# A hybrid decoder layer: condition rows ahead of the second broadcast, inputs written rounded, weights cast by GpSimd, four idle products

## The chip, the cores and the metric

The kernel runs on one core of one Trainium2 chip. The metric is the device time of one execution in microseconds, lower is better. The engines are PE (matrix products, with PEld for its weight loads), DVE (vector), ACT (scalar), POOL (GpSimd) and SP, whose queue issues the transfers.

## The reference

One layer of a hybrid decoder is applied to a prompt of 1024 tokens and to 32 sample tokens (8 sequences of 4). What the change touches is the beginning: the normalised input, scaled and shifted by rows that come from a condition vector, and its product with the input weights.

```python
def adaln_in(x, c, w_ada, b_ada, g_norm):
    mod = jax.nn.silu(c) @ w_ada + b_ada
    shift, scale, gate = jnp.split(mod, 3, axis=-1)
    h = rmsnorm(x, g_norm) * (1 + scale[:, None, :]) + shift[:, None, :]
    return h, gate[:, None, :]

def layer(x, c, ...):
    h, gate = adaln_in(x, c, w_ada, b_ada, g_norm)
    (mq, mk, mv, mi, mf, mo, mz, aq, ak, av, az, gm, ga) = split_in(h @ w_in)
    y_m, C, n, m = mlstm_branch(mq, mk, mv, mi, mf, mo, mz, ...)
    ...   # sliding-window attention of aq, ak, av gives y_a
    u = jax.nn.sigmoid(gm) * (y_m @ w_mo) + jax.nn.sigmoid(ga) * (y_a @ w_ao)
    return x + gate * (u @ w_o), ...
```

## The kernel before

The input is kept transposed: eight tiles of 128 rows of the model dimension (index k), in three parts by token: part 0 and part 1 of 512 prompt tokens each (`xT[0]`, `xT[1]`) and part 2, the 32 sample tokens (`xS`). The products run over three pieces of columns of the same tokens: 384, 384 and 288, so that piece 1 needs parts 0 and 1, and piece 2 needs part 1 and the samples.

The beginning goes as follows. `x_sq` squares the tiles (ACT or DVE) and adds the squares with products against ones (`xs`); `x_cols` brings the sums into columns (`xc`); `x_rs` forms the reciprocal root on DVE with a chain of small instructions (`xr`); `x_dg` makes diagonal tiles of it (`xdg`); `x_rows` broadcasts them over all rows by a product with ones (`xb`); `x_mul` multiplies the input by that. Beside this, the condition is multiplied by four chunks of `w_ada`, each of which serves two values of k. `ada_chunk` is a generator in steps: eight products (`ada_q`), an ACT copy of the result (`adas_q`), four small products that transpose it (`adat_q`), and `tokens_done`, which writes the scale A and the shift B on DVE.

`h_part(k, p)` then writes x*A+B on ACT, a rounded copy of it (the high half `h_h`), and on DVE the difference (the low half `h_l`). `h_samples` does the same for the samples. `split4` splits a weight tile into halves `wh` and `wl` alike. `pair(ks, p, accs)` runs the products of the first two jobs, `ak` and `av`, for piece p: for each k and job three products, high with high, high weight with low input, low weight with high input. The loop over `two` takes k in four groups of two; in each group it forms the inputs, runs the pieces 0, 1 and 2, and steps the next condition chunk in between. After it come the gate products (`gg`) and the rest of the layer.

The order on PE, DVE and ACT is the order in which the program is written: each instruction is tied to the one before it on its engine. POOL and SP are in program order as well, except that a planner moves an instruction to where its tile is free. The raw weights of the two jobs have nine tiles, and the transfers share eight semaphores, so an issue on SP waits until the one eight places ahead has landed.

Of the kernel before, what the change touches and what calls it, by code (L numbers as in the profile page):

```python
# [10 lines left out]
F32 = mybir.dt.float32  # L11
# [4 lines left out]
ALU = mybir.AluOpType  # L16
# [156 lines left out]
def body(tc, a):  # L173
    nc = tc.nc
    with ExitStack() as ctx:
# [14 lines left out]
        def po(shape, name):  # L190
            return ps.tile(shape, F32, tag="o", bufs=2, name=name)
# [61 lines left out]
        def mm(out, lhsT, rhs, start, stop, share=1, more=False):  # L253
            n = int(np.prod(rhs.shape[1:]))
            side.now += max(n, 250) / 2400 if rhs.dtype == F32R else max(n * 4 // share, 128) / 2400
            side.products += 1
            in_order(nc.tensor.matmul(out, lhsT, rhs, start=start, stop=stop, skip_group_check=more))  # L257
# [117 lines left out]
        def x_sq(cols, j, p, ks, on_v=(), apart=KT):  # L375
            n = PARTS[p][1]
            if p == 2:
                sqs = ht([128, KT, NS], "xsq2")
                S.activation(sqs, xS, AF.Square)
                for k in ks:  # L380
                    columns(cols, j, n, sqs[:, k], one[:, 0:1], k == 0, k == KT - 1)
                return
            for k in ks:
                if k == 0:
                    sums[p] = po([128, 512], f"xs{p}")
                sq = ht([128, 512], "xsq")
# [57 lines left out]
        def h_part(k, p):  # L444
            x = xT[p][k]
            hi, lo = h_hi(k, *PARTS[p]), h_lo(k, *PARTS[p])
            S.activation(x, x, AF.Identity, bias=B[:, k, 0:1], scale=A[:, k, 0:1])
            if k < 6:
                S.copy(hi, x)
            else:  # L450
                V.tensor_copy(hi, x)
            V.tensor_tensor(lo, x, hi.bitcast(F32), op=ALU.subtract)

        def h_samples(ks):
            ks = slice(ks[0], ks[-1] + 1)
            xv = xS[:, ks].rearrange("p k (b t) -> p k b t", t=NT)
            for i, m in enumerate((A, B)):
                V.tensor_tensor(xv, xv, m[:, ks, 1:9].unsqueeze(3).to_broadcast((128, ks.stop - ks.start, NB, NT)),
                                op=(ALU.mult, ALU.add)[i])
            hi, lo = (f(ks, SEQ, NS) for f in (h_hi, h_lo))  # L460
            V.tensor_copy(hi, xS[:, ks])
            V.tensor_tensor(lo, xS[:, ks], hi.bitcast(F32), op=ALU.subtract)


        def granule(name, tag, bufs, dt=F32):
# [9 lines left out]
                dma(raws[-1], src[:, 4 * i:4 * i + 4], late)  # L475
            return raws, name

        def split4(raw, name, eng=V):
            hi, lo = granule(f"wh_{name}", "wh", 4, F32R), granule(f"wl_{name}", "wl", 4, F32R)
            S.copy(hi, raw)  # L480
            eng.tensor_tensor(lo, raw, hi.bitcast(F32), op=ALU.subtract)
            return hi, lo

# [1076 lines left out]
        def pair(ks, p, accs):  # L1560
            c0, n = PIECES[p]
            for k in ks:
                for job_, acc in zip(order[:2], accs):
                    wh, wl = ready[job_]
                    o = acc[:, :n]
                    mm(o, wh(k), h_hi(k, c0, n), start=(k == 0), stop=False)
                    mm(o, wh(k), h_lo(k, c0, n), start=False, stop=False)
                    mm(o, wl(k), h_hi(k, c0, n), start=False, stop=(k == KT - 1))

        def pair_end(p, accs):  # L1570
            c0, n = PIECES[p]
            ev_ak(p, accs[0], c0, n)
            ev_av(p, accs[1], c0, n)

        two = [range(k, k + 2) for k in range(0, KT, 2)]

# [8 lines left out]
                dma(raws1[n][i], a["w1"][JOBS[n]][:, 4 * i:4 * i + 4])  # L1585

        def first_split(n, i, eng):
            parts1[n].append(split4(raws1[n][i], f"{n[0]}0_{i}", eng))
            ready[n] = tuple((lambda k, j=j: parts1[n][k // 4][j][:, k % 4]) for j in range(2))

        adas = [tokens_ada(0, "h0")]
# [1 line left out]
        adas += [tokens_ada(1, "h1"), tokens_ada(2, "l1")]  # L1593
        first_load(1)
        adas.append(tokens_ada(3))
        xc0, xc1 = po([128, 8], "xc0"), po([128, 8], "xc1")
        xc0, xc1 = pg([128, 8], "xc0"), pg([128, 8], "xc1")
        x_sq(xc0, 4, 2, range(KT))
        x_sq(xc0, 0, 0, range(KT), (1, 3, 5, 7))
        x_sq(xc1, 0, 1, range(4), (1, 3))  # L1600
        conditions()
        x_cols(xc0, 0)
        dgs = x_dg((0, 2), *x_rs((0, 2), xc0))
        x_sq(xc1, 0, 1, range(4, KT))
        x_cols(xc1, 1)
        rows = {p: x_rows(p, dgs[p]) for p in (0, 2)}
        dgs = x_dg((1,), *x_rs((1,), xc1), True)
        x_mul(2, rows[2], None)
        x_mul(0, rows[0], two[0])
        steps(adas[0], 3)  # L1610
        rows[1] = x_rows(1, dgs[1])
        kept = ht([128, 512], "xbs")
        S.copy(kept, rows[1])
        x_mul(0, rows[0], two[1])
        run(adas[0])
        first_split(order[0], 0, V)
        x_mul(1, kept, two[0][:1])
        acc = [(pg([128, 384], "g_ak0"), po([128, 384], "g_av0")),
               (po([128, 384], "g_ak1"), pg([128, 384], "g_av1")),
               (pa([128, 384], "g_ak2"), pa([128, 384], "g_av2"))]  # L1620
        for q, kk in enumerate(two):
            more = q < len(two) - 1
            if q == 2:
                attention_begin()
                wg, gbias = gate_load()
                preload(order[2])
                dma(cst[:, C_TRI:], a["cst"][:, C_TRI:])
            h_part(kk[0], 0)
            if q == 0:
                first_split(order[1], 0, V)  # L1630
            h_part(kk[1], 0)
            if q == 0:
                x_mul(1, kept, kk[1:])
            if q and more:
                steps(adas[q + 1], 2)
            pair(kk, 0, acc[0])
            if q == 0:
                steps(adas[1], 2)
            h_part(kk[0], 1)
            if q and more:  # L1640
                steps(adas[q + 1], 1)
            h_part(kk[1], 1)
            if q == 0:
                steps(adas[1], 1)
                x_mul(0, rows[0], range(4, KT))
            h_samples(kk)
            if not more:
                pair_end(0, acc[0])
                prefetch(order[2])
            pair(kk[:1], 1, acc[1])  # L1650
            if more:
                run(adas[q + 1])
            pair(kk[1:], 1, acc[1])
            if more:
                x_mul(1, kept, two[q + 1])
            else:
                pair_end(1, acc[1])
            pair(kk, 2, acc[2])
            if q == 0:
                for n in order[:2]:  # L1660
                    first_split(n, 1, V)
        pair_end(2, acc[2])
        zg = []
        for p, (c0, n) in enumerate(PARTS):
# [270 lines left out]
```

## Time and profile before

| what | value |
|---|---|
| median of 3 runs | 856.53 us (855.49 to 857.94) |
| the profiled execution, its own time | 854.31 us |
| its span | 852.5 us |
| busy share of PE, DVE, ACT, POOL | 97%, 67%, 45%, 4% |
| share of PE in the chain that ended last | 93% |
| DMA share from 0 to 62 us | 0.96 |
| granted PE clock from 0 to 62 us | 0.97 |

The span is the profiled execution from its first to its last instruction; its own time is longer by what lies around it. In a timeline each row has a start, a duration, the engine, the line of the program, the operation, and in brackets the idle time of the engine before it with what ended it. Since every operation of DVE and ACT is issued by one helper (line 219) and every product by another (line 257), groups are told apart by the names of tiles. A product in f32 has two records, so the eight products of a condition chunk show as x16. The granted clock is the share of the full clock that the throttle let through.

### The profile page before, as it was taken

What the parts mean: (1) busy time and instruction counts of PE and PEld (TensorE: products, weight loads), DVE (VectorE), ACT (ScalarE), POOL (GpSimd) and SP (SyncE); (2) the same over time, 40 slices, a digit from 0 to 9 for tenths busy, and PEclk for the clock granted to TensorE, in tenths of its full rate; (3) what the DMA queues carried; (4) which work ended last, traced back from release to release, by engine and by line L of the source; (5) the groups of instructions that cost most, each with busy time, mean ns of one, the idle gap of its engine ahead of it and who ended that gap; (6) DMA issues with size and microseconds to landing.
All of it is one profiled execution on the core that took longest, in us unless ns stands there. A gap on an engine that the chain in (4) does not pass through costs nothing.

```text
span 852.5 us, 15278 instructions
## 1 busy us (share of the span) xinstructions
PE 829.6 (97%) x5248; PEld 697.5 (82%) x5248; DVE 569.5 (67%) x1619; ACT 386.7 (45%) x987; POOL 30.9 (4%) x63
## 2 busy tenths in 40 slices
PE   6899999999999999999999999999999999999996
PEld 2689989789788988888888777777778999987785
DVE  4877785555675785656655656787877657756586
ACT  4762356546565554555444444444445232223231
POOL 0000000000000000000000000000002112220000
PEclk9999999999999999999999999999999999999998
DMA  9996548348637655273423443554435888353502
GB/s 329 361 318 226 144 141 292 108 114 292 193 92 234 171 186 170 83 226 91 137 99 110 133 131 101 147 173 125 125 112 177 267 288 301 124 160 111 174 25 80
DMA packets 114321, 146.48 MB, mean 172 GB/s; under 512 B 27088, under 2 KB 70992, under 8 KB 114212
## 3 DMA queue, kind: packets, MB, share of 16 engines
q1 hardware_dynamic: 114244, 145.52, 53.5%
q8 instruction: 41, 0.67, 0.3%
q14 instruction: 36, 0.29, 0.1%
HBM read 107.50 MB, written 38.99 MB: 172 GB/s over the span
## 4 chain that ended last, share of the span: by engine, by line
PE 93%; DVE 3%; ACT 2%; DMA 1%; issue 1%; SPq 0%; DVEq 0%
PE fo L257 11%; PE bx L257 11%; PE by L257 10%; PE bw L257 10%; PE g_aq L257 6%; PE g_w_mo L257 5%; PE bz L257 5%; PE g_w_ao L257 5%; PE g_mq L257 4%; PE g_mk L257 3%; PE g_mv L257 3%; PE sc L257 2%; PE smp L257 2%; PE oT L257 2%; PE g_ak L257 2%; PE pt L262 1%
## 5 line engine op out<-in xcount | busy, mean ns | idle before, releaser
L257 PE MATMUL g_w_ao<-ya,wh_w_ao 128*128 128x384 f32 (+1 forms) x192 | 45.6, 322 | 0.1
L257 PE MATMUL g_w_mo<-ym_l,wh_w_mo 128*128 128x384 f32 (+1 forms) x192 | 45.7, 323 | 0.0
L219 ACT ACTIVATE p<-p,nmx 128x256 f32<-128x256 f32 (+1 forms) x64 | 31.1, 488 | 20.6 <-DVE nmx L219 20.6
L219 ACT ACTIVATE fjk<-rows_l 128x512 bf16<-128x512 f32 (+2 forms) x19 | 11.6, 609 | 50.2 <-DVE rows_l L219 26.2
L219 DVE CUSTOM_DVE_ANT_0 p<-sc,cst,sink 128x256 f32<-128x256 f32 (+1 forms) x64 | 26.1, 464 | 11.9 <-PE sc L257 10.0
L257 PEld LDWEIGHTS g_w_ao<-ya,wh_w_ao 128*128 128x128 f32 x192 | 33.5, 188 | 0.6 <-DVE ya L219 0.4
L257 PEld LDWEIGHTS g_w_mo<-ym_l,wh_w_mo 128*128 128x128 f32 x192 | 33.5, 188 | 0.0
L257 PE MATMUL g_aq<-h_h,wh_aq 128*128 128x384 f32 (+1 forms) x96 | 32.5, 338 | 0.0
L257 PE MATMUL g_aq<-h_l,wh_aq 128*128 128x384 f32 (+1 forms) x96 | 31.0, 323 | 0.0
L257 PE MATMUL g_w_mo<-ym_l,wl_w_mo 128*128 128x384 f32 (+1 forms) x96 | 31.0, 323 | 0.0
L257 PE MATMUL g_aq<-h_h,wl_aq 128*128 128x384 f32 (+1 forms) x96 | 31.0, 323 | 0.0
L257 PE MATMUL g_w_ao<-ya,wl_w_ao 128*128 128x384 f32 (+1 forms) x96 | 30.8, 321 | 0.0
L257 PE MATMUL g_mk<-h_h,wh_mk 128*128 128x384 f32 (+1 forms) x72 | 24.9, 346 | 0.0
L257 PE MATMUL g_mq<-h_h,wh_mq 128*128 128x384 f32 (+1 forms) x72 | 24.8, 344 | 0.0
L257 PE MATMUL g_mk<-h_h,wl_mk 128*128 128x384 f32 (+1 forms) x72 | 23.2, 323 | 0.0
L257 PE MATMUL g_mk<-h_l,wh_mk 128*128 128x384 f32 (+1 forms) x72 | 23.2, 323 | 0.0
L257 PE MATMUL g_mq<-h_h,wl_mq 128*128 128x384 f32 (+1 forms) x72 | 23.2, 323 | 0.0
L257 PE MATMUL g_mq<-h_l,wh_mq 128*128 128x384 f32 (+1 forms) x72 | 23.2, 322 | 0.0
L219 DVE TENSOR_TENSOR fot<-fo,rows_l 128x512 f32<-128x512 f32 (+1 forms) x17 | 11.2, 657 | 15.4 <-PE fo L257 15.2
L219 DVE SCALAR_TENSOR_TENSOR u_h<-tgw_ao,g_w_ao 128x384 f32<-128x384 f32 (+1 forms) x24 | 12.3, 518 | 11.8 <-PE g_w_ao L257 11.5
L219 DVE SCALAR_TENSOR_TENSOR tgw_mo<-tgw_mo,g_w_mo 128x384 f32<-128x384 f32 (+1 forms) x24 | 12.5, 519 | 10.3 <-PE g_w_mo L257 10.3
L257 PEld LDWEIGHTS g_aq<-h_h,wh_aq 128*128 128x128 f32 x96 | 18.0, 188 | 1.4 <-issue 1.0
(1447 smaller groups left out, 2665.1 us busy)
## 6 DMA issues: line engine op xcount, KB each, us to landing
hb<-hD SPq DMA_DIRECT2D x24, 256.0 KB
x<-xT SPq DMA_DIRECT2D x16, 256.0 KB
early_h<-w_ada SPq DMA_DIRECT2D x8, 512.0 KB
hD<-x SPq DMA_DIRECT2D x16, 256.0 KB
adar_ga<-w_ada SPq DMA_DIRECT2D x16, 256.0 KB
wr_ga<-w SPq DMA_DIRECT2D x16, 256.0 KB
wr_gm<-w SPq DMA_DIRECT2D x16, 256.0 KB
taD<-gt SPq DMA_DIRECT2D x16, 256.0 KB
```

The costliest lines, as they stand in the source:

```text
L219: ins = f(*args, **kw)
L257: in_order(nc.tensor.matmul(out, lhsT, rhs, start=start, stop=stop, skip_group_check=more))
L262: in_order(nc.tensor.transpose(out, in_, idn))
```

## The change

Only the beginning is written differently. The sums of part 0 are taken ahead of the squares of part 1, and all squares of part 1 go to ACT. The first condition chunk is run to its end, with A and B, ahead of the diagonals and the broadcast of part 1; four products of ones with ones, whose result is not read, stand in front of that broadcast. `h_part` writes the high half of k = 0 and 1 directly with the scale and shift, and x by a second pass. The first weight tile of each job is cast by GpSimd, and `h_samples` runs on GpSimd. The broadcast rows of part 0 are kept in SBUF as those of part 1 were. In each group the transposes of the next chunk stand ahead of the whole of piece 1, and of the three products the second and the third are swapped.

```diff
         def h_part(k, p):
...
+            if k < 2:
+                S.activation(hi, x, AF.Identity, bias=B[:, k, 0:1], scale=A[:, k, 0:1])
             S.activation(x, x, AF.Identity, bias=B[:, k, 0:1], scale=A[:, k, 0:1])
-            if k < 6:
+            if k < 2:
+                pass
+            elif k < 6:
                 S.copy(hi, x)
...
         def h_samples(ks):
...
-                V.tensor_tensor(xv, xv, m[:, ks, 1:9].unsqueeze(3).to_broadcast((128, ks.stop - ks.start, NB, NT)),
+                G.tensor_tensor(xv, xv, m[:, ks, 1:9].unsqueeze(3).to_broadcast((128, ks.stop - ks.start, NB, NT)),
...
-            V.tensor_copy(hi, xS[:, ks])
-            V.tensor_tensor(lo, xS[:, ks], hi.bitcast(F32), op=ALU.subtract)
+            G.tensor_copy(hi, xS[:, ks])
+            G.tensor_tensor(lo, xS[:, ks], hi.bitcast(F32), op=ALU.subtract)
...
-        def split4(raw, name, eng=V):
+        def split4(raw, name, eng=V, by=S):
...
-            S.copy(hi, raw)
+            (by.copy if by is S else by.tensor_copy)(hi, raw)
...
-                    mm(o, wh(k), h_lo(k, c0, n), start=False, stop=False)
-                    mm(o, wl(k), h_hi(k, c0, n), start=False, stop=(k == KT - 1))
+                    mm(o, wl(k), h_hi(k, c0, n), start=False, stop=False)
+                    mm(o, wh(k), h_lo(k, c0, n), start=False, stop=(k == KT - 1))
...
+        def warm(n):
+            w = pb([128, 128], "warm")
+            for i in range(n):
+                mm(w, one, one, start=True, stop=True)
...
-        x_sq(xc1, 0, 1, range(4), (1, 3))
         conditions()
         x_cols(xc0, 0)
+        x_sq(xc1, 0, 1, range(4))
         dgs = x_dg((0, 2), *x_rs((0, 2), xc0))
         x_sq(xc1, 0, 1, range(4, KT))
+        rows = {p: x_rows(p, dgs[p]) for p in (0, 2)}
         x_cols(xc1, 1)
-        rows = {p: x_rows(p, dgs[p]) for p in (0, 2)}
-        dgs = x_dg((1,), *x_rs((1,), xc1), True)
-        x_mul(2, rows[2], None)
-        x_mul(0, rows[0], two[0])
+        x_mul(0, rows[0], range(1))
+        kept = [ht([128, 512], "xbs0"), None]
+        S.copy(kept[0], rows[0])
+        rs1 = x_rs((1,), xc1)
+        x_mul(0, rows[0], range(1, 2))
         steps(adas[0], 3)
+        run(adas[0])
+        dgs = x_dg((1,), *rs1, True)
+        first_split(order[0], 0, V)
+        warm(4)
         rows[1] = x_rows(1, dgs[1])
...
             if q == 0:
+                S.copy(kept[1], rows[1])
                 steps(adas[1], 1)
-                x_mul(0, rows[0], range(4, KT))
+                x_mul(2, rows[2], None)
             h_samples(kk)
...
-            pair(kk[:1], 1, acc[1])
             if more:
                 run(adas[q + 1])
-            pair(kk[1:], 1, acc[1])
+            pair(kk, 1, acc[1])
```

On PE, from the squares of part 0 (`xs`) to the first g product, the order before is this (the numbers behind names tell the tiles apart):

```order
L257 MATMUL xs_249<-xsq,one 32x512 x4
L257 MATMUL xc_210<-cst,xsum 128x1 x4
L257 MATMUL xs_249<-xsq,one 32x512 x4
L257 MATMUL xc_211<-cst,xsum 128x1 x4
L257 MATMUL xb_314<-xdg_289,one 128x128 x4
L257 MATMUL xb_319<-xdg_290,one 128x32
L257 MATMUL ada_q_345<-early_h_173,c_106 32x512 x8
L257 MATMUL xb_355<-xdg_336,one 128x128 x4
L257 MATMUL adat_q_364<-cst,adas_q_344 128x9 x4
L257 MATMUL g_ak_377<-h_h_383,wh_ak_0_372 128x384
```

And now on PE, in the same place:

```order
L257 MATMUL xc_208<-cst,xsum 128x1 x4
L257 MATMUL xs_257<-xsq,one 32x512 x8
L257 MATMUL xb_308<-xdg_287,one 128x128 x4
L257 MATMUL xb_313<-xdg_288,one 128x32
L257 MATMUL xc_209<-cst,xsum 128x1 x4
L257 MATMUL ada_q_339<-early_h_173,c_106 32x512 x8
L257 MATMUL adat_q_349<-cst,adas_q_338 128x9 x4
L257 MATMUL warm<-one 128x128 x4
L257 MATMUL xb_371<-xdg_357,one 128x128 x4
L257 MATMUL g_ak_376<-h_h_382,wh_ak_0_362 128x384
```

The column sums of part 0 moved ahead of all of part 1's squares, the broadcast of part 0 ahead of part 1's sums, and the transposes (`adat_q`) ahead of the broadcast of part 1, with the idle products between the two.

On ACT, from the copy of the first condition result (`adas_q`) to that of the second, the order before is this:

```order
L219 COPY adas_q_344<-ada_q_345 128x512
L219 COPY xbs<-xb_355 128x512
L219 CAST wh_ak_0_372<-wr_ak_0_169 128x512
L219 ACTIVATE x_0_66<-x_0_66,B,A 128x512
L219 CAST h_h_383<-x_0_66 128x512
L219 CAST wh_av_0_388<-wr_av_0_171 128x512
L219 ACTIVATE x_1_68<-x_1_68,B,A 128x512
L219 CAST h_h_383<-x_1_68 128x512
```

And now on ACT, from the same copy:

```order
L219 COPY adas_q_338<-ada_q_339 128x512
L219 ACTIVATE xdg_357<-cst,xr_y 128x128 x2
L219 ACTIVATE h_h_382<-x_0_66,B,A 128x512
L219 ACTIVATE x_0_66<-x_0_66,B,A 128x512
L219 ACTIVATE h_h_382<-x_1_68,B,A 128x512
L219 ACTIVATE x_1_68<-x_1_68,B,A 128x512
L219 ACTIVATE h_h_382<-x_0_86,B,A 128x512
L219 ACTIVATE x_0_86<-x_0_86,B,A 128x512
L219 ACTIVATE h_h_382<-x_1_88,B,A 128x512
L219 ACTIVATE x_1_88<-x_1_88,B,A 128x512
L219 COPY xbs_408<-xb_371 128x512
L219 COPY adas_q_409<-ada_q_410 128x512
```

The two weight casts and the copy of part 1's rows are gone from in front of the inputs, each input has two passes with scale and shift, and the copy of part 1's rows stands behind all four of them, ahead of the second condition copy.

On POOL there is now, behind the memset of a padded query tile, what follows (before, the next instruction there was the memset of the gate weights' tile):

```order
L727 MEMSET qpad 128x256
L484 CAST wh_ak_0_362<-wr_ak_0_169 128x512
L484 CAST wh_av_0_388<-wr_av_0_171 128x512
L462 ISA
L462 TENSOR_TENSOR xS<-xS,A 128x64
L462 TENSOR_TENSOR xS<-xS,B 128x64
L465 CAST h_h_382<-xS 128x2x32
L466 TENSOR_TENSOR h_l_383<-xS,h_h_382 128x2x32
```

The casts and the samples' four instructions are new on POOL. The row named ISA is put in by the compiler ahead of the first two-input instruction; before, it stood ahead of the first such instruction late in the program (line 1745).

More of the change, by code (lines that the diff above doesn't have):

```diff
@@ L1587, in first_split @@
         def first_split(n, i, eng):
-            parts1[n].append(split4(raws1[n][i], f"{n[0]}0_{i}", eng))
+            parts1[n].append(split4(raws1[n][i], f"{n[0]}0_{i}", eng, G if i == 0 else S))
             ready[n] = tuple((lambda k, j=j: parts1[n][k // 4][j][:, k % 4]) for j in range(2))
@@ L1595, in body @@
         adas.append(tokens_ada(3))
-        xc0, xc1 = po([128, 8], "xc0"), po([128, 8], "xc1")
         xc0, xc1 = pg([128, 8], "xc0"), pg([128, 8], "xc1")
@@ L1599, in body @@
         x_sq(xc0, 0, 0, range(KT), (1, 3, 5, 7))
-        x_sq(xc1, 0, 1, range(4), (1, 3))
         conditions()
         x_cols(xc0, 0)
+        x_sq(xc1, 0, 1, range(4))
         dgs = x_dg((0, 2), *x_rs((0, 2), xc0))
         x_sq(xc1, 0, 1, range(4, KT))
+        rows = {p: x_rows(p, dgs[p]) for p in (0, 2)}
         x_cols(xc1, 1)
-        rows = {p: x_rows(p, dgs[p]) for p in (0, 2)}
-        dgs = x_dg((1,), *x_rs((1,), xc1), True)
-        x_mul(2, rows[2], None)
-        x_mul(0, rows[0], two[0])
+        x_mul(0, rows[0], range(1))
[3 more added lines that the diff above has]
+        x_mul(0, rows[0], range(1, 2))
         steps(adas[0], 3)
+        run(adas[0])
+        dgs = x_dg((1,), *rs1, True)
+        first_split(order[0], 0, V)
+        warm(4)
         rows[1] = x_rows(1, dgs[1])
[L1612 to L1617, printed above, removed]
         acc = [(pg([128, 384], "g_ak0"), po([128, 384], "g_av0")),
@@ L1629, in body @@
             if q == 0:
+                x_mul(1, rows[1], kk[:1])
                 first_split(order[1], 0, V)
             h_part(kk[1], 0)
-            if q == 0:
-                x_mul(1, kept, kk[1:])
             if q and more:
@@ L1637, in body @@
             if q == 0:
+                x_mul(1, rows[1], kk[1:])
+                kept[1] = ht([128, 512], "xbs1")
                 steps(adas[1], 2)
+            elif more:
+                steps(adas[q + 1], 1)
+                x_mul(0, kept[0], two[q + 1])
             h_part(kk[0], 1)
-            if q and more:
-                steps(adas[q + 1], 1)
             h_part(kk[1], 1)
             if q == 0:
+                S.copy(kept[1], rows[1])
                 steps(adas[1], 1)
-                x_mul(0, rows[0], range(4, KT))
+                x_mul(2, rows[2], None)
             h_samples(kk)
+            if q == 0:
+                x_mul(0, kept[0], two[1])
+            if q == 1:
+                for n in order[:2]:
+                    first_split(n, 1, V)
             if not more:
@@ L1649, in body @@
                 prefetch(order[2])
-            pair(kk[:1], 1, acc[1])
             if more:
                 run(adas[q + 1])
-            pair(kk[1:], 1, acc[1])
+            pair(kk, 1, acc[1])
             if more:
-                x_mul(1, kept, two[q + 1])
+                x_mul(1, kept[1], two[q + 1])
             else:
@@ L1658, in body @@
             pair(kk, 2, acc[2])
-            if q == 0:
-                for n in order[:2]:
-                    first_split(n, 1, V)
         pair_end(2, acc[2])
```

## Prediction

> **What bounds the kernel now.** I read the page first, then the busy time by stretches, then the timelines of the engines from 12 to 40 us, then the queue of transfers. The page says which engine sets the time.
>
> ```profile
> span 852.5 us, 15278 instructions
> PE 829.6 (97%) x5248; PEld 697.5 (82%) x5248; DVE 569.5 (67%) x1619; ACT 386.7 (45%) x987; POOL 30.9 (4%) x63
> ```
>
> PE is busy for 97%, so an edit away from PE counts only where PE waits. The busy time by stretches shows where that is (columns: stretch, length, busy us of PE, weight load, DVE, ACT, POOL, granted clock, DMA share, GB/s).
>
> ```profile
> 20.00:24.72 4.72, 4.71 (x40) 3.01 (x38) 4.37 (x17) 2.04 (x5) 0.00 (x0) 1.00 1.02 391
> 24.72:28.26 3.54, 0.86 (x3) 0.61 (x4) 3.26 (x8) 2.97 (x5) 0.00 (x0) 1.00 1.02 408
> 28.26:31.68 3.42, 3.42 (x15) 2.50 (x17) 2.11 (x4) 3.32 (x6) 0.00 (x0) 0.50 1.02 404
> 31.68:38.30 6.62, 6.62 (x51) 5.00 (x50) 6.36 (x16) 3.74 (x7) 0.00 (x0) 1.00 1.03 383
> 62.00:852.00 790.00, 778.48 (x4926) 660.99 (x4918) 527.33 (x1497) 349.63 (x927) 30.06 (x57) 1.00 0.51 159
> ```
>
> PE has 0.86 us of work in the 3.54 us after 24.72, then runs 3.42 us at half clock, and from 31.68 on has no gap. What the change can win lies before 33 us. PE's timeline there (start, duration, operation):
>
> ```profile
> 14.95 1.05 PE L257 MATMUL xc<-cst,xsum 128*128 128x1 f32 x8
> 19.42 1.47 PE L257 MATMUL xb<-xdg,one 128*128 128x128 f32 x10
> 20.82 2.01 PE L257 MATMUL ada_q<-early_h,c 128*32 128x512 f32 x16
> 22.76 1.16 PE L257 MATMUL xb<-xdg,one 128*128 128x128 f32 x8
> 23.76 0.96 PE L257 MATMUL adat_q<-cst,adas_q 128*128 128x9 f32 x8
> 27.11 0.44 PE L257 MATMUL g_ak<-h_h,wh_ak 128*128 128x384 f32 x1 [2.40 <-ACT h_h L219]
> ...
> 31.63 1.92 PE L257 MATMUL ada_q<-early_h,c 128*32 128x512 f32 x16
> 33.48 0.45 PE L257 MATMUL g_ak<-h_h,wh_ak 128*128 128x384 f32 x1
> ...
> 34.66 0.95 PE L257 MATMUL adat_q<-cst,adas_q 128*128 128x9 f32 x8
> 35.47 0.42 PE L257 MATMUL g_ak<-h_h,wh_ak 128*128 128x384 f32 x1
> ...
> 36.61 0.29 PE L257 MATMUL g_ak<-h_h,wh_ak 128*128 128x288 f32 x1
> ```
>
> From start to start: a condition product (ada_q) takes 1.85 us, its transposes (adat_q) 0.81, a broadcast (xb) 1.0, six g products 1.18 at full clock. The first g product waits 2.40 us for h_h of ACT, and that chain, not PE, is what the change reorders.
>
> ```profile
> 12.25 0.59 ACT L219 COPY xsum<-xs 128x512 f32<-128x512 f32 x1 [1.89 <-PE xs L257]
> 14.11 2.62 ACT L219 ACTIVATE xsq<-x 128x512 f32<-128x512 f32 x4
> 22.88 0.59 ACT L219 COPY adas_q<-ada_q 128x512 f32<-128x512 f32 x1 [0.16 <-PE ada_q L257]
> 25.60 0.81 ACT L219 ACTIVATE x<-x,B,A 128x512 f32<-128x512 f32 x1 [0.54 <-DVE B L219]
> 26.44 0.62 ACT L219 CAST h_h<-x 128x512 fp32r<-128x512 f32 x1
> 27.49 0.81 ACT L219 ACTIVATE x<-x,B,A 128x512 f32<-128x512 f32 x1
> 28.33 0.62 ACT L219 CAST h_h<-x 128x512 fp32r<-128x512 f32 x1
> 53.64 2.93 ACT L219 ACTIVATE x<-x,B,A 128x512 f32<-128x512 f32 x4 [2.59 <-DVE B L219]
> ```
>
> ```profile
> 16.04 0.22 DVE L219 TENSOR_SCALAR ssq<-xc 32x1 f32<-32x1 f32 x2 [1.35 <-PE xc L257]
> 18.50 1.01 DVE L219 TENSOR_SCALAR xdg<-cst,xr_y 128x128 f32<-128x128 f32 x5
> 25.09 0.17 DVE L219 TENSOR_TENSOR A<-adat_q,b 128x18 f32<-128x18 f32 x1
> 27.09 0.69 DVE L219 TENSOR_TENSOR h_l<-x,h_h 128x512 fp32r<-128x512 f32 x1
> ```
>
> **The change part by part**, by the clock of the profiled execution.
>
> *Start.* Part 0's column sums now stand ahead of part 1's squares on PE. Its copy ends at 12.84 and the sums take 1.05, so they are there at 13.95 instead of 16.0. The reciprocal root (16.04 to 18.50) and xdg follow: 16.5 to 17.5. Part 1's squares go to ACT alone, two more of about 0.53: the last ends at 17.3 (16.73 before), PE is through with them at 17.6, and xb of part 0 runs from there to 18.7, not from 19.42. Then come part 2's small product and part 1's sums, to 20.0. The condition product is next, and here a transfer is late. A transfer on the SP queue is issued when the one eight places ahead has landed; the issue at 21.75 stands eight places behind the last quarter of the first condition weights.
>
> ```profile
> 21.75 1.00 SPq L245 DMA_DIRECT2D early_l<-w_ada  x2
> 23.09 0.33 SPq L245 DMA_DIRECT2D early_l<-w_ada  x1
> ...
> 40.53 1.53 SPq L245 DMA_DIRECT2D wr_aq<-w  x3
> ```
>
> Two of eight products are left after 21.75: it ends at 22.25 (22.83 before). The 2 us won at the start shrink to 0.6.
>
> *Condition rows ahead of the second broadcast.* The copy to SBUF (0.6) and the transposes no longer stand behind xb of part 1: transposes 23.0 to 23.9, A and B to 24.4 instead of 25.56. That is 1.15 earlier.
>
> *Inputs written rounded.* ACT writes h_h directly: 24.45 + 0.81 = 25.25, against 27.06. But xb of part 1 now stands ahead of the first g product; half of its diagonals follow B on DVE (0.4), so xb runs 24.9 to 26.0, and g starts at 26.0 against 27.11. The price comes after: x is written by a second pass that waits for the first, 0.84 + 0.71 (pitches from 25.60 to 26.44, and 2.93 for four) instead of 0.84 + 0.53. Two inputs end at 27.6, the low half of the second at 28.6, and its last products at 29.5. Twelve products are 2.2 us of work in 3.5, against 31.63 as their end now.
>
> *Four idle products.* f32 like xb's four, so at most 1.0: 23.9 to 24.9, in the wait for the diagonals. They cost nothing there. With the first xb, the sums, rows and g products, PE now has more than half its time filled from 20 to 29.5, so I take the half-clock spell as gone. [...]
>
> *Transposes of the next chunk ahead of all of piece 1.* The product runs 29.5 to 31.4. Its copy stands on ACT behind eight passes (24.45 + 4 x 1.55 + 0.1 = 30.8) and the copy of xb (to 31.4): 31.5 to 32.1. PE waits 0.7 for it, transposes to 33.0, then piece 1 (2.2) to 35.2. Before, piece 2 began at 36.61. This wait is new, and it is what is late next.
>
> *Samples and weight casts on GpSimd.* DVE loses four small instructions a chunk, ACT two casts. POOL's prices, from the groups by form:
>
> ```profile
> L1768 POOL TENSOR_TENSOR wo_l<-wo,wo_h 128x512 fp32r<-128x512 f32 x8 | 10.6, 1320 | 65.0 <-ACT wo_h L219 51.4 <-DVE wl_w_mo L219 4.6 <-DMA tgw_mo<-tmD 4.6
> L1260 POOL TENSOR_TENSOR u_h<-u_h,tgw_mo 128x384 f32<-128x384 f32 x4 | 4.1, 1013 | 8.9 <-DVE tgw_mo L219 8.9
> L1260 POOL TENSOR_TENSOR u_h<-u_h,tgw_mo 128x288 f32<-128x288 f32 x2 | 1.6, 802 | 0.7 <-DVE tgw_mo L219 0.7
> L980 POOL COPY ks<-mk 128x32 f32<-128x32 f32 x3 | 0.8, 281 | 58.0 <-ACT mk L219 37.5 <-DMA hb<-hD 20.4
> L723 POOL MEMSET qpad<- 128x256 f32 x1 | 0.3, 311 | 0.3 <-POOLq L1907 0.3
> ```
>
> No row shows a 128x512 cast on POOL. Bounds: not under the 0.31 of a 128x256 memset; above, the 281 ns of a 32-column copy less about 0.1, taken per column, makes 2.9. I take the two-input 1.32, the same width. The two first weights landed by 22.4 and 23.1 (read the same way: the second issue of the row at 21.75 starts 0.33 before its end, and the next at 23.09), so the casts end at 25.1, in time; at 2.9 each they end at 28.2, the av products begin at 28.9, and everything from there is 1.1 later. The samples' chain: 0.31 for each two-input step of 64 columns (802 less 224 columns at 2.2 ns), 0.4 for the cast, some 0.1 a wait: 1.7. Part 2's multiplication now stands behind the low halves on DVE, done at 32.1; samples at 33.8. Piece 2 wants them at 35.2: hidden, with 1.4 to spare. The later ones have more.
>
> *The rest.* The swap of the second and third product changes no count; it lets PE start before the low half is there. The g_av bank of piece 1 is freed by part 2's multiplication (32.1), before 33.0. From piece 2 on, PE has the same products as before; the last condition weights landed by 42.1 (the three issues from 40.53, of which the second waits for them) and PE asks for them at 47.03 less the gain. The SP queue moves two wr_aq issues ahead of stores, with the same bytes ahead of the gate weights. So the gain carries to the end.
>
> **Sum:** 36.61 - 35.2 = 1.4 us. The profiled execution took 854.31 (span 852.5 and 1.8 around it), so it would take 852.9; the median of the runs is 856.53, 2.2 above it, and I forecast 855.1. About 0.3%, 2.6 us, is what a measurement can tell from no change, so this is within it.
>
> **The rivals.**
>
> *First, slower: GpSimd is not ready for its first two-input instruction.* The change's order has a set-up (ISA) ahead of it, right behind the casts; before, the same set-up had the 58 us of idle time ahead of this row, so its length is not shown.
>
> ```profile
> 642.54 1.56 POOL L1745 TENSOR_TENSOR ya<-yr,ya 128x384 fp32r<-128x384 f32 x1 [58.06 <-DVE hg L219]
> 645.15 1.01 POOL L1745 TENSOR_TENSOR ya<-yr,ya 128x384 fp32r<-128x384 f32 x1 [1.04 <-ACT ya L219]
> ```
>
> The first one took 0.55 more than the next; more may be hidden. Place: piece 2 of the first chunk. Point: set-up up to 35.2 - 1.7 - 25.1 = 8.4 us is hidden, or 6.4 with the dear casts, which put piece 2 at 36.3 and their own end at 28.2; beyond, each us is one of PE's. For it: it would run while transfers fill the engines (DMA share 1.02 above). Against: the casts may be cheap. At 12 us PE waits 3.6, then a spell as at 28.26 costs 1.7: -1.4 + 3.6 + 1.7 = +3.9, 860.4. [...] Chance 0.27.
>
> *Second: the half-clock spell stays.* For it: PE waits 0.7 twice and 1.3 inside piece 0. Against: no stretch is as empty as 0.86 in 3.54. It costs 1.0 in piece 0, where half is hidden by ACT, or 1.7 later: net -0.4 to +0.3, about 856.4. Chance 0.15.
>
> *Third, faster: the runs that are timed lose more to the clock than the profiled one* (they are 2.2 us longer), say a second spell of 1.7 of which most goes too: -1.4 - 1.5 = -2.9, 853.6. Against: nothing shows a second one. Chance 0.14.
>
> **How the numbers follow.** The forecast has 0.44. Only the third rival is faster by over 0.3% (0.14), only the first slower (0.27); the forecast and the second are within (0.59). The range runs from 853.0, below the third, to 860.5, the first at 12 us; it takes in the dear casts (856.2). Left out is a longer set-up.
>
> **What would show it.** Right: first g product near 26.0, next condition product near 29.5, piece 2 near 35.2, clock 1.00 throughout, POOL's samples done by 34. Wrong: POOL's first two-input instruction starting after 33.5 with PE idle before piece 2; a stretch at 0.50; a condition copy on ACT later than 32.

## The result, and the profile after

The changed kernel takes 855.16 us in the median of 22 runs (853.89 to 856.62), the kernel before 856.54 (22 runs beside them). The ratio is 0.9988 with a 95% interval of 0.998 to 0.9995, a gain of 0.4 to 1.7 us, smaller than the 0.3% that was called no change. The forecast was 855.1. The number fits, in part by luck: the profile shows that two of its terms were wrong and made up for each other. One of the twelve runs of the kernel without idle products, below, took 1646 us, a slow one, and is left out of its ratio and mean clock.

The page and the busy time by stretches of the changed kernel, in the stretches that were shown of before:

```profile
span 853.6 us, 15307 instructions
...
PE 832.7 (98%) x5256; PEld 697.7 (82%) x5256; DVE 565.7 (66%) x1601; ACT 387.8 (45%) x988; POOL 42.2 (5%) x81
```

```profile
24.72:28.26 3.54, 2.86 (x25) 2.69 (x24) 1.86 (x7) 2.22 (x5) 1.02 (x2) 1.00 1.02 406
28.26:31.68 3.42, 2.12 (x12) 1.48 (x11) 2.80 (x5) 3.35 (x5) 0.00 (x0) 1.00 1.02 407
31.68:38.30 6.62, 5.91 (x43) 4.16 (x42) 5.21 (x12) 4.56 (x8) 3.19 (x6) 1.00 1.04 391
```

No stretch is at 0.50 any more: PE has 2.86 us of records in the 3.54 after 24.72, where it had 0.86. Yet this profiled span is 1.1 us longer than that of before (852.5). PE's timeline tells where the gain stayed:

```profile
13.81 1.05 PE L257 MATMUL xc<-cst,xsum 128*128 128x1 f32 x8 [0.68 <-ACT xsum L219]
...
19.70 1.49 PE L257 MATMUL xb<-xdg,one 128*128 128x128 f32 x10
...
22.10 2.79 PE L257 MATMUL ada_q<-early_h,c 128*32 128x512 f32 x16
25.57 1.06 PE L257 MATMUL adat_q<-cst,adas_q 128*128 128x9 f32 x8 [0.68 <-ACT adas_q L219]
...
28.31 0.42 PE L257 MATMUL g_ak<-h_h,wh_ak 128*128 128x384 f32 x1
...
29.63 0.45 PE L257 MATMUL g_ak<-h_l,wh_ak 128*128 128x384 f32 x1 [0.72 <-DVE h_l L219]
...
30.83 0.45 PE L257 MATMUL g_av<-h_h,wl_av 128*128 128x384 f32 x1 [0.58 <-DVE wl_av L219]
...
32.43 1.92 PE L257 MATMUL ada_q<-early_h,c 128*32 128x512 f32 x16
35.06 1.06 PE L257 MATMUL adat_q<-cst,adas_q 128*128 128x9 f32 x8 [0.71 <-ACT adas_q L219]
...
38.17 0.29 PE L257 MATMUL g_ak<-h_h,wh_ak 128*128 128x288 f32 x1
```

The first condition product ends at 24.89, where it ended at 22.83; piece 2 starts at 38.17 instead of 36.61. From the one to the other it is 13.28 us now and was 13.78. I use this distance, called the middle below, because what stands ahead of it differs from trace to trace (with all transfers the first condition product ends at 22.58 to 24.89), and the two ends of it are read in every trace. POOL's timeline in the changed kernel:

```profile
24.52 0.61 POOL L484 CAST wh_ak<-wr_ak 128x512 fp32r<-128x512 f32 x1 [23.46 <-DMA wr_ak<-w]
...
34.81 0.68 POOL L462 TENSOR_TENSOR xS<-xS,A 128x64 f32<-128x64 f32 x1 [9.01 <-DVE xS L219]
35.57 0.63 POOL L462 TENSOR_TENSOR xS<-xS,B 128x64 f32<-128x64 f32 x1
...
36.58 0.83 POOL L466 TENSOR_TENSOR h_l<-xS,h_h 128x64 fp32r<-128x64 f32 x1
```

GpSimd's first two-input instruction waited for part 2's rows of DVE (done at 34.73), not for a set-up, and its four instructions end at 37.41, 0.76 ahead of piece 2.

### The profile page after: what moved, and what is told of

It is laid out like the page before. It is cut to its first block, busy times and chain, and to the rows that moved or that the text cites. A ratio compares the mean times of both kernels' runs of the same rounds, so it can differ in the third digit from the quotient of the medians.

```text
span 853.6 us, 15307 instructions
## 1 busy us (share of the span) xinstructions
PE 832.7 (98%) x5256; PEld 697.7 (82%) x5256; DVE 565.7 (66%) x1601; ACT 387.8 (45%) x988; POOL 42.2 (5%) x81
## 4 chain that ended last, share of the span: by engine, by line
PE 93%; ACT 2%; DVE 2%; DMA 1%; issue 1%; SPq 0%; DVEq 0%
PE fo L257 11%; PE bx L257 11%; PE by L257 10%; PE bw L257 10%; PE g_aq L257 6%; PE g_w_mo L257 5%; PE bz L257 5%; PE g_w_ao L257 5%; PE g_mq L257 4%; PE g_mk L257 4%; PE g_mv L257 3%; PE sc L257 2%; PE smp L257 2%; PE oT L257 2%; PE pt L262 2%; PE g_ak L257 1%
```

## The experiments

The times and mean granted clocks of all kernels stand here together; the sections speak of them. Kernels of one group ran on one chip and share the runs of before (35, 34 and 29 of them, medians 855.81, 856.04 and 855.42, mean clock 0.9937, 0.9935 and 0.9936). "Middle" is read from each kernel's one trace.

| group | kernel | median us | ratio to before, 95% | mean clock | first condition product ends | middle |
|---|---|---|---|---|---|---|
| - | before (profile) | - | - | - | 22.83 | 13.78 |
| - | changed, 22 runs | 855.16 | 0.9988 (0.998 to 0.9995) | 0.9970 | 24.89 | 13.28 |
| 1 | no idle products | 856.67 | 1.0002 (0.9986 to 1.0018) | 0.9938 | 23.23 | 15.22 |
| 1 | inputs formed as before | 855.42 | 0.9988 (0.9976 to 1.0) | 0.9962 | 23.67 | 13.11 |
| 1 | no GpSimd | 855.81 | 0.9994 (0.9981 to 1.0007) | 0.9972 | 24.51 | 13.46 |
| 1 | transposes between | 855.56 | 0.9989 (0.9976 to 1.0002) | 0.9968 | 23.69 | 12.49 |
| 2 | before + idle products | 854.23 | 0.9985 (0.997 to 1.0) | 0.9961 | 24.11 | 12.92 |
| 2 | both waits out | 854.78 | 0.9989 (0.9979 to 0.9999) | 0.9965 | 23.75 | 12.33 |
| 2 | changed, less load | 854.75 | 0.9994 (0.9983 to 1.0005) | 0.9966 | 22.98 | 13.30 |
| 2 | before, less load | 856.17 | 1.0004 (0.9994 to 1.0015) | 0.9932 | 23.49 | 13.40 |
| 3 | before + idle + casts | 854.87 | 0.9992 (0.9979 to 1.0004) | 0.9952 | 23.46 | 12.09 |
| 3 | changed again | 855.24 | 0.9997 (0.9986 to 1.0007) | 0.9966 | 23.87 | 13.27 |
| 3 | before + idle products again | 854.19 | 0.9989 (0.9979 to 1.0) | 0.9969 | 22.58 | 12.99 |

### The idle products taken out

```diff
-        warm(4)
```

> The changed kernel without its four idle products. I compare the stretch from the end of the first condition product to the start of piece 2 (13.28 us in the changed kernel's profile, 13.78 in that of before), since transfers shift everything ahead of it. Theory: the half-clock spell is gone because the transposes and the broadcast now follow each other (2.15 us of work in the 3.4 us after the condition product, against 0.86 in 3.54 before), so the idle products are not needed: no stretch at 0.50, 13.2 to 13.4 us, time as the changed kernel within 0.3 us. Rival: it is the idle products that keep the clock. Then a stretch near 0.50 comes back in piece 0 and the stretch to piece 2 grows by 1.0 to 1.7 us, to 14.3 to 15.0.

The rival was right, and beyond its range of 14.3 to 15.0. The busy time by stretches, and PE's timeline:

```profile
23.23:26.64 3.41, 1.94 (x16) 1.85 (x16) 3.09 (x12) 2.33 (x5) 0.65 (x1) 1.00 1.03 412
26.64:33.46 6.82, 6.37 (x23) 3.90 (x25) 5.18 (x9) 5.71 (x8) 0.29 (x1) 0.50 1.02 399
```

```profile
25.76 1.33 PE L257 MATMUL xb<-xdg,one 128*128 128x128 f32 x8 [0.76 <-DVE xdg L219]
...
32.05 2.59 PE L257 MATMUL ada_q<-early_h,c 128*32 128x512 f32 x16
```

After 1.94 us of records in 3.41, PE runs 6.82 us at half clock, and the middle is 15.22. Over the runs the mean clock falls back to 0.9938, that of before: none of the eleven has more than 0.996, while 25 of the 36 runs of the other three kernels of the group have 0.997 or 0.998. So the new order does not fill the gap; the four products do. The clock shows it, the times alone do not: this kernel's mean is 0.6 us above that of the other three, with a 95% interval of -0.2 to 1.4.

### The idle products alone

Eight products of ones with ones behind the first chunk's transposes, all else as before:

```diff
         run(adas[0])
+        w = pb([128, 128], "warm")
+        for i in range(8):
+            mm(w, one, one, start=True, stop=True)
```

> The kernel before with nothing but eight idle products (ones with ones) behind the first chunk's transposes, in the gap in front of the first g product. Theory: they keep the clock at 1.00 in piece 0. Its twelve products then end when the second input's low half allows, about 30.6 instead of 31.63, so the stretch from the end of the first condition product to piece 2 falls from 13.78 to 12.7 to 13.0 us and the time by 0.8 to 1.0: as much as the whole change gains, and the new order by itself gains nothing. Rival: piece 0 is set by ACT and not by the clock; then the stretch stays at 13.6 to 13.9 and the time within 0.3 us of before.

The middle is 12.92, within the theory's 12.7 to 13.0. PE's timeline and the stretches of this trace:

```profile
26.16 2.03 PE L257 MATMUL warm<-one 128*128 128x128 f32 x16
...
28.36 0.44 PE L257 MATMUL g_ak<-h_h,wh_ak 128*128 128x384 f32 x1 [0.18 <-ACT h_h L219]
```

```profile
21.28:24.69 3.41, 3.41 (x19) 1.08 (x12) 3.27 (x11) 1.22 (x3) 0.00 (x0) 0.50 1.02 375
69.07:72.48 3.41, 3.41 (x13) 3.31 (x12) 2.68 (x13) 0.47 (x2) 0.00 (x0) 0.50 0.93 267
```

Piece 0 keeps the full clock (1.00 from 28.28 to 31.66). This execution had half-clock spells in two other places; over its runs the mean clock is 0.9961. The median is 1.8 us below that of before, more than the 0.8 to 1.0 that was expected and at least as much as the whole change gains.

### The same two side by side

> The changed kernel once more, on the same chip as the next one. By the runs so far the idle products give the whole gain and the rest of the change nothing or a loss of up to 0.8 us: the changed kernel should be 0.4 to 1.0 us slower than the kernel before with the idle products alone, at the same mean clock (0.9965 to 0.997). Rival: the rest of the change brings something of its own; then it is at least as fast.

> The kernel before with eight idle products once more: mean clock 0.996, 1.2 to 1.7 us faster than before if the first measurement (854.45 against 855.92 in the mean) holds. Rival: that one was chance; then 0 to 0.6 us faster.

PE's timeline of the changed kernel again, and then of before with the idle products, both at full clock from start to piece 2:

```profile
18.92 1.49 PE L257 MATMUL xb<-xdg,one 128*128 128x128 f32 x10
...
21.33 2.54 PE L257 MATMUL ada_q<-early_h,c 128*32 128x512 f32 x16
...
37.14 0.29 PE L257 MATMUL g_ak<-h_h,wh_ak 128*128 128x288 f32 x1
```

```profile
19.20 1.47 PE L257 MATMUL xb<-xdg,one 128*128 128x128 f32 x10
...
20.60 1.98 PE L257 MATMUL ada_q<-early_h,c 128*32 128x512 f32 x16
...
35.57 0.30 PE L257 MATMUL g_ak<-h_h,wh_ak 128*128 128x288 f32 x1
```

With the clock out of the way the new order is 1.57 us later at piece 2: 1.29 at the end of the first condition product (23.87 against 22.58), 0.28 in the middle. In the runs the means differ by 0.75 us (855.30 and 854.55, 95% interval of the difference -0.17 to 1.65), at nearly one mean clock; the runs with a clock of 0.998 alone have 854.39 (6 runs) and 853.84 (7). That the rest of the change costs something is therefore likely by the runs, and shown only in these two traces; by the interval, it brings at most 0.2 us of its own. The second measurement of the idle products is 1.2 us below before by the medians and 1.1 by the means, at the lower end of what was expected.

### The inputs formed as before, and no GpSimd

```diff
-            if k < 2:
-                S.activation(hi, x, AF.Identity, bias=B[:, k, 0:1], scale=A[:, k, 0:1])
             S.activation(x, x, AF.Identity, bias=B[:, k, 0:1], scale=A[:, k, 0:1])
-            if k < 2:
-                pass
-            elif k < 6:
+            if k < 6:
```

> The changed kernel with the inputs formed as before (x in one pass with scale and shift, then a rounded copy). In the changed kernel the first g product starts when the second broadcast ends (28.31), 0.33 after h_h was there (27.18 and 0.8 of duration). With the copy behind the pass h_h is there at 28.6. Theory: the broadcast hides half of it, the first g product is 0.3 us later, the eight passes of ACT end 0.4 earlier, and from the second condition product on nothing differs: 13.0 to 13.5 us from the first condition product to piece 2. Rival: writing rounded is what the gain rests on; then the 0.62 of a copy is added in full: 13.9.

The middle is 13.11, as the theory said: the first g product waits 0.24 for h_h, and the next condition product comes earlier in return. The reason is a price of the two passes: in the changed kernel DVE's low half waits 0.74 for the second pass over x, and PE 0.72 for the low half (at 29.63 in its timeline above); here that wait is gone. Writing the inputs rounded brings nothing.

```diff
-                G.tensor_tensor(xv, xv, m[:, ks, 1:9]...
+                V.tensor_tensor(xv, xv, m[:, ks, 1:9]...
...
-            G.tensor_copy(hi, xS[:, ks])
-            G.tensor_tensor(lo, xS[:, ks], hi.bitcast(F32), op=ALU.subtract)
+            V.tensor_copy(hi, xS[:, ks])
+            V.tensor_tensor(lo, xS[:, ks], hi.bitcast(F32), op=ALU.subtract)
...
-            parts1[n].append(split4(raws1[n][i], f"{n[0]}0_{i}", eng, G if i == 0 else S))
+            parts1[n].append(split4(raws1[n][i], f"{n[0]}0_{i}", eng, S))
```

> The changed kernel with the two weight casts back on ACT and the samples' four instructions back on DVE. Theory: ACT sets the pace from the condition copy to the end of piece 0, so the two casts of 0.62 stand in its chain: the first cast delays the first h_h by 0.62, of which 0.33 is hidden, the second all that follows, so the second condition product starts 0.6 to 1.2 us later and piece 2 with it: 13.9 to 14.5 us. Rival: GpSimd's part is neutral, because the low halves on DVE set the pace; then 13.1 to 13.5 and the time of the changed kernel.

The rival was right, with 13.46. The first cast falls into a wait that ACT has anyway, for B:

```profile
25.64 0.60 ACT L219 CAST wh_ak<-wr_ak 128x512 fp32r<-128x512 f32 x1
26.81 0.82 ACT L219 ACTIVATE h_h<-x,B,A 128x512 fp32r<-128x512 f32 x1 [0.56 <-DVE B L219]
```

### The two new waits taken out

The transposes back in the middle of piece 1:

```diff
+            pair(kk[:1], 1, acc[1])
             if more:
                 run(adas[q + 1])
-            pair(kk, 1, acc[1])
+            pair(kk[1:], 1, acc[1])
```

> The changed kernel with the transposes of each next chunk back in the middle of piece 1 (behind its first six products, as before). Theory: the 0.71 us that PE waits for the second condition copy is covered by six products of piece 1, and nothing takes its place: 12.5 to 12.7 us from the first condition product to piece 2, the whole 0.6 us faster than the changed kernel. Rival: the low half of piece 1's first input (DVE, behind the weights' low halves) ends the wait instead; then PE waits for that, and 13.0 to 13.4.

The middle is 12.49 and the transposes wait for nothing: the theory's step. Its end of "the whole 0.6 us faster" doesn't show in the times (855.56, interval up to 1.0002). Then the low half of the second weight ahead as well, with the transposes in the middle as in the edit above:

```diff
-        first_split(order[0], 0, V)
+        for n in order[:2]:
+            first_split(n, 0, V)
...
-                first_split(order[1], 0, V)
```

> The changed kernel with the transposes back in the middle of piece 1 and the low halves of both first weights on DVE ahead of the inputs' low halves. Theory: both waits of PE that the change brought, 0.71 for the condition copy and 0.58 for the low weights of av, go: 12.0 to 12.4 us from the first condition product to piece 2, 1.0 to 1.2 us faster than the changed kernel. Rival: the second low weight (0.8 on DVE) now delays the first input's low half by as much, and only the first wait goes: 12.6 to 12.8.

The middle is 12.33, in the theory's range. The times again don't show it: 854.78 is 0.4 to 0.5 below the two medians of the changed kernel (855.16 and 855.24, other groups), not 1.0 to 1.2. PE's timeline: the wait for wl_av is gone, and one of 0.72 for the first low half stays.

```profile
28.50 0.45 PE L257 MATMUL g_ak<-h_l,wh_ak 128*128 128x384 f32 x1 [0.72 <-DVE h_l L219]
...
34.13 0.95 PE L257 MATMUL adat_q<-cst,adas_q 128*128 128x9 f32 x8
...
36.08 0.29 PE L257 MATMUL g_ak<-h_h,wh_ak 128*128 128x288 f32 x1
```

### Less to load

```diff
-                for k in range(0, KT, 2):
+                n = KT // 2 if chunk == 0 else KT
+                for k in range(0, n, 2):
                     dma(home[:, k:k + 2], a["w_ada"][chunk, :, k:k + 2])
-                return [home[:, k] for k in range(KT)]
+                return [home[:, k % n] for k in range(KT)]
```

> The changed kernel without the transfer of the second half of the first condition weights (1 MB); the first half is multiplied in its place, so the work on the engines is the same. Theory: the end of the first condition product is set by that transfer, and what the new order wins ahead of it (2 us in the prediction) is lost there. Without it PE reaches the product with its operands landed, it takes 1.85 us without a wait, and the kernel gains 1.5 to 2.5 us. Rival: the engines' own chain sets it; then under 0.5 us.

> The same edit in the kernel before. Theory: there PE reaches the product later (20.82, behind the first broadcast), so the transfer costs it less, and the kernel gains only 0 to 0.6 us; the changed kernel with this edit is then 2 to 3 us faster than the one before with it, against 1.4 with all transfers. Rival: both gain alike, since the later chunks come earlier too; then the difference between the two stays at 1.0 to 1.6.

The theory fell. The kernel before gains nothing (856.17 against 856.04), and the changed kernel with less to load is 1.3 us below before, no more than it is with everything loaded; the two are 1.4 apart, as the second rival had it, and their mean clocks are those of the kernels with and without idle products. In the changed kernel the product no longer waits for a transfer, and still ends at 22.98, 0.9 earlier than in the side-by-side trace:

```profile
18.66 1.49 PE L257 MATMUL xb<-xdg,one 128*128 128x128 f32 x10
...
21.06 1.92 PE L257 MATMUL ada_q<-early_h,c 128*32 128x512 f32 x16
```

PE reaches the product at 21.06 without a transfer in the way, where the prediction had 20.0. Its own chain is a second bound there, next to the transfer.

### The length of GpSimd's set-up

```diff
+                probe = cp.tile([128, 16], F32, name="probe")
+                G.tensor_tensor(probe, one[:, 0:16], one[:, 16:32], op=ALU.mult)
```

> The changed kernel with one more instruction on GpSimd: a product of two constant tiles (128x16) right behind the two weight casts, so that the first two-input instruction waits for nothing but GpSimd itself. In the changed kernel the first one started at 34.81, 9.0 us behind the casts' end, but there it waited for part 2's rows, so 9.0 is only an upper bound of the set-up. [...] Rival: nothing stands there; the small product starts within 0.5 us.

The planner put the small product at the start of the program instead, so that it is the first two-input instruction there. Of this kernel there is one execution, the profiled one. POOL's timeline:

```profile
0.74 0.31 POOL L727 MEMSET qpad<- 128x256 f32 x1 [0.29 <-POOLq L1922]
1.36 0.22 POOL L1642 TENSOR_TENSOR probe<-one 128x16 f32<-128x16 f32 x1 [0.31 <-DVE one L219]
```

It answers the question for that place only: the product starts 0.31 us after the memset ends, and that wait is put down to DVE's tile of ones. A set-up between the two takes no more than 0.31 us (anything that was done ahead of the first row would not show). The middle is 13.30, that of the changed kernel.

### The idle products with GpSimd's casts

```diff
-            S.copy(hi, raw)
+            (by.copy if by is S else by.tensor_copy)(hi, raw)
...
-            parts1[n].append(split4(raws1[n][i], f"{n[0]}0_{i}", eng))
+            parts1[n].append(split4(raws1[n][i], f"{n[0]}0_{i}", eng, G if i == 0 else S))
...
+        w = pb([128, 128], "warm")
+        for i in range(8):
+            mm(w, one, one, start=True, stop=True)
```

> The kernel before with the eight idle products and, from the change, only the two first weight casts on GpSimd. Theory: the idle products keep the clock (mean granted clock of the runs 0.996 to 0.997 against 0.9936 of before), and the two casts of 0.62 leave ACT's chain in front of the two first inputs: 0.3 to 0.8 us faster than the idle products alone. Rival: the copy of the broadcast rows and the low halves on DVE set the pace; then the same time as the idle products alone within 0.3 us.

In the trace the middle falls to 12.09, 0.9 less than with the idle products alone. The runs don't show it (854.87 against 854.19), with a lower mean clock, 0.9952 against 0.9969, so the clock was not kept as the theory had it. Why is open, and the shorter middle isn't shown to be a gain.

## Why the prediction was right, and where not

**The start: wrong, in two steps.** The sums of part 0 came where I put them: their product starts at 12.87 to 13.81 in the traces with the new order, and the reciprocal root follows. The first failed step is "the last ends at 17.3, PE is through with them at 17.6, and xb of part 0 runs from there". ACT's and PE's rows in the second trace of the changed kernel:

```profile
13.47 0.26 ACT L219 ACTIVATE ct<-cT 128x72 f32<-128x72 f32 x1 [0.60 <-DMA cT<-cT]
13.64 4.25 ACT L219 ACTIVATE xsq<-x 128x512 f32<-128x512 f32 x8
```

```profile
14.31 4.68 PE L257 MATMUL xs<-xsq,one 128*32 128x512 f32 x16 [0.33 <-ACT xsq L219]
```

The condition's first step (`ct`), which now stands ahead of part 1's squares on ACT, waits 0.60 for its transfer, so the squares end at 17.89 and not at 17.3. PE is through 1.1 us later, at 18.99, because the last product starts only when the last square is there. The same 1.1 was to be read in the trace of before, where the last square ended at 16.73 and the last product ran from 16.79 to 17.83:

```profile
15.93 1.90 PE L257 MATMUL xs<-xsq,one 128*32 128x512 f32 x8
```

I took 0.3 for it. xb thus runs from 18.92, about where it was. Part 1's sums now stand between it and the condition product, so PE comes to that at 21.33, against 20.60 in the kernel before with idle products.

The second failed step is "Two of eight products are left after 21.75: it ends at 22.25", which takes 0.5 for what follows the last transfer. The issue eight places behind that transfer, in the same trace:

```profile
22.79 0.33 SPq L245 DMA_DIRECT2D early_l<-w_ada  x1
```

The condition product ends at 23.87, 1.08 behind this issue. In the trace of before the two are 21.75 and 22.83, again 1.08: there the transfer set the end already, so by that trace an earlier PE wins nothing at this place. Five of the eight traces with the new order and all transfers end 1.07 to 1.08 behind the issue, as do the three with the order of before, all transfers and full clock there; in the other three PE's own 1.92 ends later than that. The product ends at 23.23 to 24.89 in the eight, and at 22.58 to 23.46 in the three: on the average of these traces, the 0.6 that I had as won is about 0.9 lost, because the transfer lands later (see below, open) and PE's own chain comes later too.

**The middle: the gain is there, and smaller.** I had 35.2 less 22.25, 12.95, for it; it is 13.28. The first g product comes 3.42 behind the condition product, where I had 3.75; piece 0 takes 4.12 from there to the next condition product, where I had 3.5; the rest is as forecast, with the eight ACT passes and the 0.7 us wait for the condition copy (0.71). What is late in piece 0 is the wait of 0.58 for wl_av, which I had not seen and which stands on DVE behind a multiplication; with both waits out, piece 0 takes 3.78:

```profile
29.49 0.68 DVE L219 TENSOR_TENSOR x<-x,xb 128x512 f32<-128x512 f32 x1
30.09 0.68 DVE L219 TENSOR_TENSOR wl_av<-wr_av,wh_av 128x512 fp32r<-128x512 f32 x1
```

**The half-clock spell: gone, as I took it**, but for another reason than mine. I argued that PE has "more than half its time filled". That is not enough: without the idle products PE has 1.94 of 3.41 us filled, and the spell comes back at twice the length; in the first trace of the idle products alone 2.75 of the 3.41 us ahead of 21.28 are filled, and a spell follows. The four products, which I took to cost nothing and to add little, are the cause (middle 13.28 with them, 15.22 without). The half was my own estimate: no trace shows a share of busy time at which the clock falls. What the traces show is the length: a spell is 3.41 us, two in a row are 6.82, and the spells of one execution start whole multiples of 3.41 us apart (last section).

**GpSimd: mis-sized twice, hidden both times.** The cast takes 0.61 and not 1.32; the two-input steps of the first chunk take 0.63 to 0.83 and not 0.31, so the samples' chain is 2.6 and not 1.7. With 0.76 to spare nothing came of it.

**The rivals.** The first, GpSimd not ready, did not come: its first two-input instruction started 0.08 us after its input, and the one trace that could show a set-up leaves at most 0.31 us for it, at the start of the program. No trace shows that the row named ISA is a set-up, or a length for it; the 12 us were a point that I picked. The second, that the spell stays, holds for a kernel that wasn't asked about, the one without idle products. The third is right in what it said of the runs and wrong in its size. The profiled execution of before had a mean clock of 0.995; its 98 runs have 0.9936, and none is above 0.996. Of the 34 runs of the changed kernel with a clock, 22 have 0.997 or 0.998. Among the runs of before the time falls by 0.55 us for each 0.001 of clock, so 0.0033 more clock is worth 1.8 us, an estimate: the mean clock also counts the end of the program, where PE has no product (from 844.6 us on in the trace of before) and the clock falls to 0.50 at 847.4 without a price. The order of the work gives part of that back: the two kernels with idle products differ by 0.75. The rest, about 1 us, lies between the 0.2 and 1.4 that the medians of its two measurements show. The number of the forecast came out of 1.4 us with other parts: more from the clock, nothing from the order. That the parts add up to it is luck.

**Open.** In the traces with the new order the last quarter of the first condition weights lands later (the issue eight places behind it is at 21.86 to 23.81, against 21.28 to 22.38 with the order of before and all transfers). The two ranges overlap, and no experiment separates a cause from chance.

## What to carry to other kernels

Where PE pauses for a few microseconds, look at the clock of the stretch behind the pause first: eight idle products in the pause were worth the whole of a reordering here (1.8 and 1.2 us by the medians, against 1.4), and are a few lines. The chain of partial sums ended one whole product after its last input here (1.1 us in the traces of before and of the changed kernel), so count that product when you move such a chain. Where an engine and a transfer bound the same step, read both ends before you count on a gain: here the transfer already set it. When a gain is a fifth of a per cent, compare the granted clock of all runs, since one profile shows one execution (before: 0.995 in the profiled one, 0.989 to 0.996 in the runs).

## What the runs showed that I had not expected

The half-clock spells keep a beat within an execution, in the three traces that show two of them apart ahead of 840 us. The stretches of before with less to load, and of the kernel with both waits out:

```profile
27.89:31.30 3.41, 3.37 (x9) 2.86 (x10) 2.74 (x5) 3.35 (x6) 0.00 (x0) 0.50 1.02 398
68.85:72.26 3.41, 3.41 (x13) 3.31 (x12) 2.65 (x14) 0.47 (x2) 0.00 (x0) 0.50 0.58 207
```

```profile
14.58:17.99 3.41, 3.41 (x14) 1.24 (x14) 2.88 (x17) 3.21 (x7) 0.00 (x0) 0.50 1.00 318
69.19:72.60 3.41, 3.41 (x14) 3.31 (x13) 2.69 (x13) 0.43 (x2) 0.00 (x0) 0.50 0.80 267
```

From the first spell to the second it is 40.96 us, 54.61, and 47.79 with the idle products alone: 12, 16 and 14 times the 3.41 us of a spell, to within 0.05 us. The first spell's place differs by kernel and execution (14.58, 21.28, 27.89; the second trace of the idle products alone has none from 12 to 845), and the mean clock of runs of one kernel, that of before, spreads from 0.989 to 0.996. In three of the eight traces with the new order and all transfers a spell starts at 14.58 to 15.1, ahead of the middle. The spell near 69 comes in three traces. Ahead of it PE's records have no gap, but two microseconds of them are products of 8 columns; PE's timeline of the kernel with both waits out, and of before, which has the same products and no spell there:

```profile
66.66 2.01 PE L257 MATMUL gp<-cst,zg 128*128 128x8 f32 x18
...
69.25 0.52 PE L257 MATMUL g_aq<-h_h,wh_aq 128*128 128x384 f32 x1
```

```profile
66.11 2.01 PE L257 MATMUL gp<-cst,zg 128*128 128x8 f32 x18
...
69.20 0.34 PE L257 MATMUL g_aq<-h_h,wh_aq 128*128 128x384 f32 x1
```

In the 3.41 us ahead of the spell PE's records are busy for 3.41, with the idle products alone and with both waits out, and the clock falls all the same. What it follows is thus not the busy time of the records alone, and these runs don't say what it is.
